# The first expert layer of a two-block model: up products of one expert between the two halves of the down products of the expert in front of it

## The chip, the cores and the metric

One core of one Trainium2 chip runs the whole program. The metric is the device time of one execution in microseconds; several executions are shown, and one more was taken with the hardware profiler.

## The reference

The program computes two transformer-like blocks on 512 tokens of width 1024, with a second stream of 256 context tokens. The change concerns one piece, the expert layer behind the first mixer of the second block (layer 0), which runs over both streams:

```python
def expert_choice_ffn(h, router, w1, w3, w2):
    B, T, D = h.shape
    cap = max(1, EC_FACTOR * T // N_EXPERTS)
    aff = jax.nn.softmax(jnp.einsum('btd,de->bte', h, router).astype(jnp.float32), -1)
    gate, idx = lax.top_k(jnp.swapaxes(aff, 1, 2), cap)
    xs = jax.vmap(lambda hb, ib: hb[ib])(h, idx)
    hid = jax.nn.silu(jnp.einsum('becd,edf->becf', xs, w1)) * jnp.einsum('becd,edf->becf', xs, w3)
    ys = jnp.einsum('becf,efd->becd', hid, w2) * gate[..., None].astype(h.dtype)
    return jax.vmap(lambda yb, ib: jnp.zeros((T, D), yb.dtype).at[ib.reshape(-1)].add(yb.reshape(-1, D)))(ys, idx)
```

There are 16 experts, each with three 1024 x 1024 fp32 matrices. With 512 tokens each expert takes cap = 64 of them, with 256 context tokens 32. The result is scaled by a modulation gate and added to the residual. All arithmetic is fp32.

## The kernel before, in words

`moe` (L1432) builds one expert layer and is called twice: for layer 0 with two token groups, group 0 with cap 64 and group 1 with cap 32 (L2601), and for layer 1 with group 0 alone (L2620). The change touches layer 0.

**Weights.** Each expert has 12 parts of 1 MB: a quarter q of w1, w3 and w2 each. `load` (L1452) issues them on SyncE's queue in the order of the list `todo` (L1441), into 14 slots that are used in turn; a load waits until both groups have used the part that was in its slot. `load(12*e + 36)` at the head of each expert names the parts that may be issued by then.

**One expert.** `up` (L1607) multiplies a quarter of w1 and w3 with the tokens xT, `act` (L1619) makes silu(h1)*h3 of the result with ScalarE and VectorE, `turned` (L1634) transposes that on TensorE and copies it to hT with ScalarE (L1640), `down` (L1643) multiplies hT with a quarter of w2 into yb, and `collect` (L1658) takes yb out: group 0 with two operations of VectorE (L1669), group 1 with four copies of ScalarE (L1672, L1673) and two additions of VectorE (L1674). Group 0's products use 64 columns of TensorE, two of them side by side; group 1's use 32, four side by side. In the trace each fp32 product is two records. h is group 0's result of the up products, hc that of group 1, and both groups' down products are yb (128\*64 for group 0, 128\*32 for group 1).

**Around the experts.** The tokens of 2 experts of group 0 (4 of group 1) are gathered together: `fetch` (L1463) finds them with a product (L1473) and an indirect DMA on POOL's queue, `turn` (L1559) transposes them into xT (L1567, evicted on L1571 and L1573), and `scatter` (L1575) brings their results back to the tokens' places: yh on ScalarE (L1588), yl and back on VectorE (L1590, L1594), products with them on TensorE (L1599), and an addition to the residual on VectorE (L1601). The scatter is a generator; `beside.step()` and `beside.drain()` run it in pieces during the up products of the next expert.

**The order.** Inside an expert the two groups are staggered: the up products run h0, h1, hc0, h2, hc1, h3, hc2 (the digit is the quarter), then act and transposes of group 0, hc3 and the act of group 1, the down products of group 0 with the transposes of group 1 in front of its third quarter, and the down products of group 1 two quarters behind. The program's order is a priority and not the order of execution: a planner goes through it once when the program is built, places on each engine the first instruction in that order whose operands are ready by its own estimate, and gives out buffers as they come free. The order that results on each engine is fixed, and is what the trace shows; this order of instructions is called the list in what follows. All products, transposes and scatters share 8 PSUM banks.

```python
            for q in range(4):
                ups(q, 0)
                if late:
                    ups(q - 1, 1)
                if q > 1:
                    beside.step()
            th = act(0, G[0])
            beside.drain()
```

Of the kernel before, what the change touches and what calls it, by code (L numbers as in the profile page):

```python
# [10 lines left out]
F32 = mybir.dt.float32  # L11
F32R = mybir.dt.float32r
BF16 = mybir.dt.bfloat16
I32 = mybir.dt.int32
# [6 lines left out]
D = 1024  # L21
# [140 lines left out]
class Feed:  # L162
# [16 lines left out]
    def load(self, upto):  # L179
        nc = self.k.nc  # L180
        while len(self.raws) < min(upto, len(self.specs)):
            src, n, w = self.specs[len(self.raws)]
            raw = self.tl("raw", F32, self.nraw, n, w)
            nc.sync.dma_start(raw, src.rearrange("(k p) c -> p k c", p=128))
            self.raws.append(raw)
# [787 lines left out]
def seg(t):  # L973

    return slice(t * 128, t * 128 + 128)
# [453 lines left out]

def moe(k, layer, groups, mods, psum, es, nslot, extra, out=None, side="right"):  # L1432

# [2 lines left out]
    bank = lambda nm="ps": psum.tile([128, 512], F32, name=nm, tag="ps")  # L1438
    dp = k.pool(f"md{layer}", 1, DRAM, es)
    parts = [("w1", 0), ("w3", 0), ("w1", 1), ("w3", 1), ("w1", 2), ("w3", 2), ("w1", 3), ("w3", 3), ("w2", 0), ("w2", 1), ("w2", 2), ("w2", 3)]  # L1440
    todo = [(e, nm, q) for e in range(16) for nm, q in parts]  # L1441
    W, pools, G, made = {}, [], [], {}

    alone = len(groups) == 1
# [18 lines left out]
    def fetch(g, gi, a):  # L1463

        n, ne, cap = g["n"], g["ne"], g["cap"]
        b = bank()
        w = 1 if alone else n
        for t in range(0, n, w):
            oh = pf.tile([128, w, ne, cap], F32, name="oh", tag=f"oh{gi}", bufs=1 + alone)
            nc.vector.tensor_tensor(oh, iota[:, :cap].unsqueeze(1).unsqueeze(1).to_broadcast([128, w, ne, cap]),  # L1470
                                    g["pos"][:, t:t + w, a * ne:a * ne + ne].unsqueeze(3).to_broadcast([128, w, ne, cap]), op=ALU.is_equal)
            for i in range(w):
                nc.tensor.matmul(b[:, :ne + 1], oh[:, i].rearrange("p e c -> p (e c)"), g["ext"][:, t + i, a], start=(t + i == 0), stop=(t + i == n - 1))  # L1473
        ii = pf.tile([128, 1], I32, name="ii", tag=f"ii{gi}", bufs=2)
        nc.vector.tensor_copy(ii, b[:, 0:1])
        xs = pf.tile([128, D], F32, name="xs", tag="xs", bufs=len(groups))
        nc.gpsimd.indirect_dma_start(out=xs, out_offset=None, in_=g["xh"][:, :],  # L1477
                                     in_offset=bass.IndirectOffsetOnAxis(ap=ii[:, 0:1], axis=0))
        sl = pf.tile([128, ne + 1], F32, name="sl", tag=f"sl{gi}", bufs=2)
        nc.vector.tensor_copy(sl, b[:, :ne + 1])  # L1480
        gate = pf.tile([128, 1], F32, name="gt", tag=f"gt{gi}", bufs=2)
        for e in range(ne):
            nc.vector.tensor_scalar(gate[e * cap:e * cap + cap], sl[e * cap:e * cap + cap, 1 + e:2 + e], 0.5, None, ALU.mult)
        return dict(xs=xs, sl=sl, gate=gate)
# [149 lines left out]
    def turned(gi, g, th):  # L1634
        m = 2 * g["cap"]
        b = bank()
        hT = p.tile([128, 4, m], F32, name="hT", tag=f"th{gi}" if alone else f"hT{gi}", bufs=1)
        for c in range(4):
            nc.tensor.transpose(b[:, c * m:c * m + m], th[:, seg(c)], k.id[:m, :m])
        nc.scalar.copy(hT.rearrange("p c m -> p (c m)"), b[:, :4 * m])  # L1640
        return hT
# [13 lines left out]
                    o, first, last = 64 * dh + 32 * (i % 2), i < 2, i > 5  # L1655
                nc.tensor.matmul(yb[o:o + cap], lhs, w[:, j, dh * 512:dh * 512 + 512], start=first, stop=last, tile_position=(0, o))  # L1656

    def collect(e, gi, g, yb):  # L1658

        cap = g["cap"]  # L1660
        ei = e % g["ne"]
        if ei == 0:
            cur[gi]["ys"] = p.tile([128, D], F32, name="ys", tag=f"ys{gi}", bufs=1)
        ys = cur[gi]["ys"]
        so = slice(ei * cap, ei * cap + cap)
        for dh in range(2):
            ds_ = slice(dh * 512, dh * 512 + 512)
            if cap == 64:
                nc.vector.tensor_tensor(ys[so, ds_], yb[64 * dh:64 * dh + 64], g["gate"][so, ds_], op=ALU.mult)  # L1669
            else:  # L1670
                t = p.tile([128, 512], F32, name="yt", tag="yt", bufs=1)
                nc.scalar.copy(ys[so, ds_], yb[64 * dh:64 * dh + 32])  # L1672
                nc.scalar.copy(t[so], yb[64 * dh + 32:64 * dh + 64])  # L1673
                nc.vector.tensor_tensor(ys[so, ds_], ys[so, ds_], t[so], op=ALU.add)  # L1674

    def run():
        nonlocal rp, pf, pq, p, iota, tid, one, hb
        slots()
        rp = k.pool(f"mr{layer}", 1, None, es)
        iota = rp.tile([128, 128], F32, name="iota")  # L1680
        nc.gpsimd.iota(iota, pattern=[[1, 128]], base=0, channel_multiplier=0, allow_small_or_imprecise_dtypes=True)
        tid = rp.tile([128, 6], F32, name="tid")
        nc.gpsimd.iota(tid, pattern=[[128, 6]], base=0, channel_multiplier=1, allow_small_or_imprecise_dtypes=True)
        for gi, g in enumerate(G):
            g["gate"] = mods.gate(g["r"], 1, rp, f"g2{layer}{gi}")
        if extra:
            pools.append(k.pool(f"mv{layer}", 1, None, es))
        load(nslot + extra - (2 if extra else 6))
        pf = k.pool(f"mf{layer}", 1, None, es)
        with ExitStack() as e2:  # L1690
            pq = k.pool(f"mq{layer}", 1, None, e2, "left")
            one = pq.tile([16, 512], F32, name="one")
            nc.gpsimd.memset(one, 1.0)
            chosen = [choose(gi, g) for gi, g in enumerate(G)]
            while any(g is None for g in nxt):
                for c in chosen:
                    next(c, 0)
        load(nslot + extra, nc.gpsimd)
        load(24)
        p = k.pool(f"mx{layer}", 1, None, es)  # L1700
        for gi, g in enumerate(G):
            turn(g, gi, nxt[gi])
        for e in range(16):
            load(12 * e + 36)
            for gi, g in enumerate(G):
                if e % g["ne"] == 0:
                    cur[gi] = nxt[gi]
            hb = [[bank("h1"), bank("h3")] if g["cap"] == 64 else [bank("hc")] for g in G]
            ybs, hTs, late = [bank("yb") for _ in G], [None] * len(G), len(G) - 1

            def ups(q, gi):
                if 0 <= q < 4:
                    up(e, q, gi, G[gi])

            def downs(q, gi):
                if 0 <= q < 4:
                    down(e, q, gi, G[gi], hTs[gi], ybs[gi])
# [10 lines that stand above are left out]
            for gi, g in enumerate(G):  # L1728
                if e % g["ne"] == g["ne"] - 2 and e < 16 - 2:
                    nxt[gi] = fetch(g, gi, e // g["ne"] + 1)  # L1730
            hTs[0] = turned(0, G[0], th)
            if late:
                ups(3, 1)
                th = act(1, G[1])
            for q in range(4 + 2 * late):
                downs(q, 0)
                if late and q == 1:
                    hTs[1] = turned(1, G[1], th)
                if late:
                    downs(q - 2, 1)  # L1740
                if q == 1:
                    for gi, g in enumerate(G):
                        if e % g["ne"] == g["ne"] - 1 and e < 15:
                            turn(g, gi, nxt[gi])
            for gi, g in enumerate(G):
                collect(e, gi, g, ybs[gi])
                if e % g["ne"] == g["ne"] - 1:
                    beside.add(scatter(g, cur[gi], e == 15))
        beside.drain()
        es.close()  # L1750

    rp = pf = pq = p = iota = tid = one = hb = None
    cur, nxt = [None] * len(groups), [None] * len(groups)
    beside = Side()
# [825 lines left out]
def whole(tc, I, out):  # L2580
    nc = tc.nc
    with ExitStack() as es:
        k = K(tc, I, es)
        setup(k)
        psum = k.pool("ps", 8, PSUM)
# [3 lines left out]
        mods = [Mods(k, i, mp, dr) for i in range(2)]  # L2589
# [8 lines left out]
        c = k.pool("xc", 1, None, ex, "left").tile([128, 2, D], F32, name="cres")  # L2598
        nc.sync.dma_start(c, I["ctx_2"][0].rearrange("(t p) d -> p t d", p=128))
        xt, ct = [x[:, t] for t in range(4)], [c[:, t] for t in range(2)]  # L2600
        first = moe(k, 0, [(0, xt, 64), (1, ct, 32)], mods[0], psum, ExitStack(), 14, 0, side="left")  # L2601
        def both(p):
            for a in range(2):
                yield from mods[1].make(psum, p, 128, 6, a)
# [44 lines left out]
```

## Time and profile before

| | us |
|---|---|
| Runs shown | 3454.38, 3463.92, 3468.79 (median 3463.92) |
| Profiled execution, its own time | 3452.15 |
| Span of the profiled execution | 3450.3 |
| First expert layer, first up product to last down product | 1523.2 to 2135.5 |

The span runs from the first to the last instruction of the profiled execution; its own time is 1.85 us longer. Times in the rows are us from the start of the span unless they say ns. In a row of the timeline the columns are start, duration from the first start to the last end, engine, line and operation, the tile written and those read, shape, and the number of records that follow one another without another group between; a bracket gives the idle time of the engine before it and what ended it. PE is TensorE, DVE VectorE, ACT ScalarE, POOL GpSimd, SPq the queue of SyncE. A later block's start less an earlier one's is the time that the earlier one took, since ends of products are modelled.

### The profile page before, as it was taken

How to read it: one execution, taken by the hardware profiler on the slowest of the kernel's cores; microseconds unless marked ns; L12 is line 12 of the kernel's file. 1: busy time of each engine (PE TensorE's matmuls, PEld its weight loads, DVE VectorE, ACT ScalarE, POOL GpSimd, SP SyncE). 2: the span in 40 equal slices, each digit the busy share in tenths (PEclk: the TensorE clock that was granted, in tenths of full speed). 3: DMA queues.
4: the chain of work that ended last, by engine and by line, in shares of the span. 5: the costliest groups of instructions: out<-in, count | busy, mean ns of one | idle time of the engine just before them, and what ended most of it. 6: DMA issues, size and time to landing. Idle time of an engine off the chain costs nothing.

```text
span 3450.3 us, 52389 instructions
## 1 busy us (share of the span) xinstructions
PE 3103.6 (90%) x21072; PEld 2032.6 (59%) x21072; DVE 1538.3 (45%) x3435; ACT 1013.0 (29%) x2175; POOL 975.3 (28%) x859
## 2 busy tenths in 40 slices
PE   8999999998989899979999999899768579699888
PEld 6898778886768666743333333687647467333322
DVE  3233544414378687342323334331577776332212
ACT  4333333322212454211111212222557443011000
POOL 5342434332323552410000000424646344000000
PEclk9999999999989999979999999899879779899999
DMA  4121122225257232178888884343222234799998
GB/s 145 61 74 49 62 74 70 66 68 166 93 158 203 81 101 65 49 304 339 333 341 334 333 339 166 105 140 117 80 59 71 66 96 154 311 409 409 409 409 349
DMA packets 372552, 625.94 MB, mean 181 GB/s; under 512 B 43998, under 2 KB 240525, under 8 KB 372310
## 3 DMA queue, kind: packets, MB, share of 16 engines
q1 hardware_dynamic: 367190, 603.58, 49.2%
q0 software_dynamic: 5120, 19.01, 1.5%
q8 instruction: 167, 2.74, 0.3%
q14 instruction: 75, 0.61, 0.1%
HBM read 596.61 MB, written 25.91 MB: 180 GB/s over the span
## 4 chain that ended last, share of the span: by engine, by line
PE 73%; DVE 11%; DMA 8%; ACT 4%; issue 2%; POOL 2%; SPq 1%; POOLq 0%; DVEq 0%; ACTq 0%
PE ps L102 11%; PE h L1617 10%; PE ps L103 10%; PE ps L104 10%; PE yb L1656 7%; DMA w<-in_moe_w_dram 6%; PE hc L1617 4%; PE ps L1599 2%; PE ps L926 1%; PE ob L762 1%; PE ps L2253 1%; DVE acc L1100 1%; DVE pr L2308 1%; DVE N L2309 1%; PE ob L1303 1%
## 5 line engine op out<-in xcount | busy, mean ns | idle before, releaser
L201 POOL TENSOR_TENSOR wlo<-wraw,whi 128x1024 fp32r<-128x1024 f32 (+5 forms) x219 | 426.8, 1970 | 755.2 <-ACT whi L197 736.5
L1617 PE MATMUL h<-w,xT 128*64 128x512 f32 x2048 | 462.6, 597 | 23.7 <-DMA w<-in_moe_w_dram 18.1
L1617 PEld LDWEIGHTS h<-w,xT 128*64 128x64 f32 x2048 | 141.1, 137 | 335.0 <-issue 253.9
L1656 PE MATMUL yb<-w,hT 128*64 128x512 f32 (+1 forms) x1536 | 301.0, 599 | 17.8 <-ACT hT L1640 15.4
L197 ACT CAST whi<-wraw 128x2048 fp32r<-128x2048 f32 (+4 forms) x108 | 161.5, 1495 | 235.7 <-PE ps L103 111.8
L1477 POOL DMA_INDIRECT xs<-xh,ii x20 | 21.3, 1067 | 728.9 <-DVE sl L1480 708.6
L1625 DVE SCALAR_TENSOR_TENSOR th<-th,h 128x512 f32<-128x512 f32 x32 | 22.0, 688 | 413.3 <-ACT th L1624 413.3
L1656 PEld LDWEIGHTS yb<-w,hT 128*64 128x64 f32 (+1 forms) x1536 | 87.2, 128 | 197.3 <-issue 153.6
L102 PE MATMUL ps<-hT,whi 128*128 128x512 f32 x416 | 171.2, 412 | 0.0
L102 PE MATMUL ps<-whi,hT 128*128 128x512 f32 (+1 forms) x424 | 164.3, 388 | 4.9 <-DVE hT L316 2.7
L103 PE MATMUL ps<-hT,wlo 128*128 128x512 f32 x416 | 166.3, 400 | 0.0
L1624 ACT ACTIVATE th<-h 128x512 f32<-128x512 f32 x32 | 19.1, 597 | 499.7 <-PE h L1617 499.7
L104 PE MATMUL ps<-hT,whi 128*128 128x512 f32 x416 | 165.7, 398 | 0.0
L103 PE MATMUL ps<-whi,hT 128*128 128x512 f32 (+1 forms) x424 | 156.4, 369 | 0.0
L104 PE MATMUL ps<-wlo,hT 128*128 128x512 f32 (+1 forms) x424 | 154.5, 367 | 0.0
L115 POOL TENSOR_TENSOR rs<-rs_t,mhalf 128x8 f32<-128x8 f32 (+3 forms) x78 | 94.7, 1218 | 113.5 <-DVE rs_t L110 93.7
L1617 PE MATMUL hc<-w,xT 128*32 128x512 f32 x1024 | 124.2, 598 | 0.0
L1669 DVE TENSOR_TENSOR ys<-yb,g 64x512 f32<-64x512 f32 x64 | 44.1, 688 | 177.5 <-PE yb L1656 177.0
L102 PEld LDWEIGHTS ps<-whi,hT 128*128 128x128 f32 x424 | 104.3, 246 | 14.5 <-DVE hT L316 3.2
L103 PEld LDWEIGHTS ps<-whi,hT 128*128 128x128 f32 x424 | 104.6, 247 | 6.4 <-issue 1.9
L1100 DVE SCALAR_TENSOR_TENSOR acc<-glu,w,acc 128x798 f32<-128x798 f32 x90 | 106.6, 1221 | 1.0
L104 PEld LDWEIGHTS ps<-wlo,hT 128*128 128x128 f32 x424 | 103.9, 246 | 5.2 <-issue 0.2
(810 smaller groups left out, 6831.4 us busy)
## 6 DMA issues: line engine op xcount, KB each, us to landing
w<-in_moe_w_dram SPq DMA_DIRECT2D x376, 1024.0 KB
wraw<-in_w_in_dram SPq DMA_DIRECT2D x48, 1024.0 KB
aw<-in_ada_w_dram SPq DMA_DIRECT2D x192, 256.0 KB
wraw<-in_od_w_in_dram SPq DMA_DIRECT2D x27, 512.0 KB
rows<-rw_rows SPq DMA_DIRECT2D x48, 192.0 KB
w<-in_moe_w_dram POOLq DMA_DIRECT2D x8, 1024.0 KB, 10.0
xh<-xn SPq DMA_DIRECT2D x10, 512.0 KB
wraw<-in_w_proj_b_dram SPq DMA_DIRECT2D x4, 1024.0 KB
```

The source lines that it names most:

```text
L102: nc.tensor.matmul(out, L[0], R[0], start=start, stop=False)
L103: nc.tensor.matmul(out, L[1], R[0], start=False, stop=False)
L104: nc.tensor.matmul(out, L[0], R[1], start=False, stop=stop)
L115: nc.gpsimd.tensor_tensor(out, t, mh.to_broadcast(list(ss.shape)), op=ALU.pow)
L197: nc.scalar.copy(hi, raw)
L201: eng.tensor_tensor(lo[:, a:b], raw[:, a:b], hi[:, a:b].bitcast(F32), op=ALU.subtract)
L762: nc.tensor.matmul(ob[pp, m * 128:m * 128 + 128], vs[a], pT[:, 2 * j + a], start=(a == 0), stop=(a == 1))
L1100: v.scalar_tensor_tensor(acc[:, c], glu[:, c, j:j + W], w2[:, j, c:c + 1], acc[:, c], ALU.mult, ALU.add)
L1599: nc.tensor.matmul(b, back, y[:, hs], start=(i == 0), stop=(i == len(terms) - 1))
L1617: nc.tensor.matmul(bb[o:o + cap], lhs, w[:, kk % 2, fh * 512:fh * 512 + 512], start=(kk == 0), stop=(kk == 7), tile_position=(0, o))
L1656: nc.tensor.matmul(yb[o:o + cap], lhs, w[:, j, dh * 512:dh * 512 + 512], start=first, stop=last, tile_position=(0, o))
L1669: nc.vector.tensor_tensor(ys[so, ds_], yb[64 * dh:64 * dh + 64], g["gate"][so, ds_], op=ALU.mult)
```

## The change

For layer 0 `moe` is called with `apart=True`. Then the expert loop is replaced by `staggered`, which runs 17 rounds. Round e has, in this order: the up products of expert e, quarter by quarter, both groups in step; the activations of both; the fetch for the next tokens and the rest of a scatter; quarters 2 and 3 of the down products of expert e-1 in step, and its collect; the transposes of both groups of expert e; quarters 0 and 1 of its down products; and the transposes of the next tokens where they are due. The weights' list follows that order of use: w1 and w3 of e, quarters 2 and 3 of w2 of e-1, quarters 0 and 1 of w2 of e. hT has two buffers, and ii, sl and the gate of the gathered tokens three. `collect` is given the gathered tokens it belongs to.

```diff
-def moe(k, layer, groups, mods, psum, es, nslot, extra, out=None, side="right"):
+def moe(k, layer, groups, mods, psum, es, nslot, extra, out=None, side="right", apart=False):
...
+    if apart:
+        todo = []
+        for e in range(17):
+            todo += [(e, nm, q) for nm, q in parts[:8] if e < 16] + [(e - 1, "w2", q) for q in (2, 3) if e] + [(e, "w2", q) for q in (0, 1) if e < 16]
...
-        ii = pf.tile([128, 1], I32, name="ii", tag=f"ii{gi}", bufs=2)
+        ii = pf.tile([128, 1], I32, name="ii", tag=f"ii{gi}", bufs=2 + apart)
...
-        hT = p.tile([128, 4, m], F32, name="hT", tag=f"th{gi}" if alone else f"hT{gi}", bufs=1)
+        hT = p.tile([128, 4, m], F32, name="hT", tag=f"th{gi}" if alone else f"hT{gi}", bufs=2 if apart else 1)
...
-        for e in range(16):
+        if apart:
+            staggered()
+        for e in range(0 if apart else 16):
...
+    def staggered():
+
+        nonlocal hb
+        before = None
+        for e in range(17):
+            load(12 * e + 36)
+            if e < 16:
+                for gi, g in enumerate(G):
+                    if e % g["ne"] == 0:
+                        cur[gi] = nxt[gi]
+                hb = [[bank("h1"), bank("h3")] if g["cap"] == 64 else [bank("hc")] for g in G]
+                for q in range(4):
+                    for gi, g in enumerate(G):
+                        up(e, q, gi, g)
+                    if q > 1:
+                        beside.step()
+                th = [act(gi, g) for gi, g in enumerate(G)]
+                for gi, g in enumerate(G):
+                    if e % g["ne"] == g["ne"] - 2 and e < 16 - 2:
+                        nxt[gi] = fetch(g, gi, e // g["ne"] + 1)
+            beside.drain()
+            if before:
+                hTs, ybs, cs = before
+                for q in (2, 3):
+                    for gi, g in enumerate(G):
+                        down(e - 1, q, gi, g, hTs[gi], ybs[gi])
+                for gi, g in enumerate(G):
+                    collect(e - 1, gi, g, cs[gi], ybs[gi])
+                    if (e - 1) % g["ne"] == g["ne"] - 1:
+                        beside.add(scatter(g, cs[gi], e == 16))
+            if e < 16:
+                hTs = [turned(gi, g, th[gi]) for gi, g in enumerate(G)]
+                ybs = [bank("yb") for _ in G]
+                before = hTs, ybs, list(cur)
+                for q in (0, 1):
+                    for gi, g in enumerate(G):
+                        down(e, q, gi, g, hTs[gi], ybs[gi])
+                for gi, g in enumerate(G):
+                    if e % g["ne"] == g["ne"] - 1 and e < 15:
+                        turn(g, gi, nxt[gi])
...
-        first = moe(k, 0, [(0, xt, 64), (1, ct, 32)], mods[0], psum, ExitStack(), 14, 0, side="left")
+        first = moe(k, 0, [(0, xt, 64), (1, ct, 32)], mods[0], psum, ExitStack(), 14, 0, side="left", apart=True)
```

## Rows read from the trace of the kernel before

**Rows 1.** The page: length of the profiled span.
```profile
span 3450.3 us, 52389 instructions
```
**Rows 2.** Windows: busy time of each engine from first up to last down product.
```profile
core 0: us, PE busy (x) PEld busy (x) DVE busy (x) ACT busy (x) POOL busy (x), PEclk, DMA share, GB/s
1523.20:2135.50 612.30, 599.43 (x3486) 204.77 (x3485) 172.93 (x337) 108.07 (x196) 18.30 (x13) 1.00 0.84 322
```
**Rows 3.** Timeline of TensorE: expert 1, and the first block of expert 2.
```profile
1559.79 7.09 PE L1617 MATMUL h<-w,xT 128*64 128x512 f32 x32
1566.81 1.94 PE L1617 MATMUL hc<-w,xT 128*32 128x512 f32 x16
1568.68 3.65 PE L1617 MATMUL h<-w,xT 128*64 128x512 f32 x16
...
1577.71 3.66 PE L1617 MATMUL hc<-w,xT 128*32 128x512 f32 x32
1581.31 0.66 PE L1639 MATMUL ps<-cc,th 128*128 128x128 f32 x4
1582.64 7.08 PE L1656 MATMUL yb<-w,hT 128*64 128x512 f32 x30 [0.67 <-ACT hT L1640]
1589.65 0.46 PE L1639 MATMUL ps<-cc,th 64*128 64x64 f32 x4
1590.04 1.09 PE L1567 MATMUL ps<-cc,xs 128*128 128x128 f32 x8
1591.06 4.64 PE L1656 MATMUL yb<-w,hT 128*64 128x512 f32 x34
1595.63 0.65 PE L1617 MATMUL h<-w,xT 128*64 128x512 f32 x2
```
**Rows 4.** Waits in 1523 to 2150: us in total, times, longest us.
```profile
PE yb L1656 <- ACT hT L1640: 8.6, 13, 0.8
```
**Rows 5.** Timeline of TensorE: end of expert 0's up products; last torn block.
```profile
1544.01 1.90 PE L1617 MATMUL hc<-w,xT 128*32 128x512 f32 x6
1545.85 0.65 PE L1639 MATMUL ps<-cc,th 128*128 128x128 f32 x4
1546.43 1.92 PE L1617 MATMUL hc<-w,xT 128*32 128x512 f32 x10
...
2130.89 4.64 PE L1656 MATMUL yb<-w,hT 128*64 128x512 f32 x34
```
**Rows 6.** Timeline of TensorE: scatter waits of expert 12, hT wait of expert 14.
```profile
2010.70 0.74 PE L1599 MATMUL ps<-yh,back 128*128 128x512 f32 x2 [1.06 <-ACT yh L1588]
2011.80 0.73 PE L1599 MATMUL ps<-yh,back 128*128 128x512 f32 x2 [0.35 <-DVE back L1594]
...
2088.67 7.08 PE L1656 MATMUL yb<-w,hT 128*64 128x512 f32 x30 [0.75 <-ACT hT L1640]
```
**Rows 7.** Timeline of all engines: ScalarE's collect copies, then transposes and hT, expert 5.
```profile
1714.56 7.09 PE L1617 MATMUL h<-w,xT 128*64 128x512 f32 x32
1714.69 0.57 ACT L1672 COPY ys<-yb 32x512 f32<-32x512 f32 x1 [6.81 <-PE yb L1656]
...
1715.88 0.58 ACT L1672 COPY ys<-yb 32x512 f32<-32x512 f32 x1
...
1736.07 0.66 PE L1639 MATMUL ps<-cc,th 128*128 128x128 f32 x4
...
1736.77 0.58 ACT L1640 COPY hT<-ps 128x512 f32<-128x512 f32 x1
```
**Rows 8.** Timeline of all engines: the end of the layer, first scatter operand and product.
```profile
2133.43 1.15 ACT L1588 ACTIVATE yh<-ys,gt 128x1024 fp32r<-128x1024 f32 x1 [2.06 <-DVE ys L1669]
...
2135.47 1.21 PE L1599 MATMUL ps<-yh,back 128*128 128x512 f32 x4
```
**Rows 9.** Waits of SyncE's queue in 1470 to 2150: us in total, times, longest us.
```profile
SPq L1458 <- PE hc L1617: 333.6, 61, 49.6
```
**Rows 10.** The instructions of the tile w, its last line: time of one load.
```profile
DMA to landing us min/median/max: 6.0/10.0/16.6
```

More of the change, by code (lines that the diff above doesn't have):

```diff
@@ L1478, in fetch @@
                                      in_offset=bass.IndirectOffsetOnAxis(ap=ii[:, 0:1], axis=0))
-        sl = pf.tile([128, ne + 1], F32, name="sl", tag=f"sl{gi}", bufs=2)
+        sl = pf.tile([128, ne + 1], F32, name="sl", tag=f"sl{gi}", bufs=2 + apart)
         nc.vector.tensor_copy(sl, b[:, :ne + 1])
-        gate = pf.tile([128, 1], F32, name="gt", tag=f"gt{gi}", bufs=2)
+        gate = pf.tile([128, 1], F32, name="gt", tag=f"gt{gi}", bufs=2 + apart)
         for e in range(ne):
@@ L1656, in down, with collect @@
                 nc.tensor.matmul(yb[o:o + cap], lhs, w[:, j, dh * 512:dh * 512 + 512], start=first, stop=last, tile_position=(0, o))
-    def collect(e, gi, g, yb):
+    def collect(e, gi, g, c, yb):
         cap = g["cap"]
@@ L1662, in collect @@
         if ei == 0:
-            cur[gi]["ys"] = p.tile([128, D], F32, name="ys", tag=f"ys{gi}", bufs=1)
-        ys = cur[gi]["ys"]
+            c["ys"] = p.tile([128, D], F32, name="ys", tag=f"ys{gi}", bufs=1)
+        ys = c["ys"]
         so = slice(ei * cap, ei * cap + cap)
@@ L1745, in run @@
             for gi, g in enumerate(G):
-                collect(e, gi, g, ybs[gi])
+                collect(e, gi, g, cur[gi], ybs[gi])
                 if e % g["ne"] == g["ne"] - 1:
```

## Prediction

> **What bounds the kernel now.** I read the page first, for the span [rows 1], then the windows for the stretch of the first expert layer [rows 2], then TensorE's instructions in order of time within it. [...] So TensorE bounds the layer, and what counts is how its 38.3 us per expert (612.3/16) are made up.
>
> One expert without a scatter shows it [rows 3]: from 1559.79 to 1595.63, 35.84 us. Two blocks of the same shape differ by 16 records and 3.44 us (7.09 - 3.65); two products of group 0 (64 columns each) run side by side, so that is 8 slots of 0.43 us. A slot of group 1 holds four records. A block of 32 takes 7.02 us to the next block's start, that is 16 x 0.43 + 0.14; a block of 16 of group 1 takes 1.87, 4 x 0.43 + 0.15. So each change of shape costs some 0.14 us beside the slots, and the order of the groups is not free. This expert has six such blocks in its up products and three in its down products.
>
> Three things in it are waste. After the transposes of group 0 (line 1639) TensorE waits 0.67 us for ScalarE's copy hT; in the whole layer that is 8.6 us in 13 waits [rows 4]. The down products of group 0 come as x30 and, behind the transposes of group 1, x34: a pair was torn, and two products run alone. x30 takes 7.02 us to the next start, as a full x32 does, and x34 takes 4.57 where 1 + 8 slots and two changes would be 4.15; on both sides together 18 slots of group 0 were used for 16, 0.86 us. Twelve experts are torn like that, the last at 2130.89, and the first expert's up products of group 1 once: 6 records take 1.84 us, four slots, and the other 10 four more, where 16 need four: 1.7 us [rows 5]. And in three experts (4, 8, 12) TensorE waits 1.06 + 0.35 us for the scatter's operands [rows 6].
>
> **What the change removes.** With the down products of the expert in front (its second half) standing behind the up products, the activations of both groups have some 5.7 us of cover (4 blocks: 12 slots x 0.43 + 4 x 0.14), the two transposes can stand together, and the scatter's waits have other work. If all three wastes go: 8.6 + 12 x 0.86 + 1.7 + 3 x 1.41 = 24.8 us. This is the most that can come off, because the products, transposes, scatters and fetches are all still there.
>
> **What it adds in changes of shape.** Group 0 and group 1 now alternate at each quarter: 8 blocks in the up products, 4 + 4 in the down products, 16 instead of 9. 7 x 16 experts x 0.14 = 15.7 us. Between 0 (the list merges blocks again, a rival) and 17.9 (at 0.16, if the small blocks pay more) I take 15.7, from [rows 3]. [...]
>
> **The wait that takes the place of the old one.** hT of group 0 is now made right after the collect of the expert in front. In the profile, ScalarE's copies of group 1's yb begin 0.13 us after the last down product and follow at 0.60 us each (1714.69 to 1715.88 for two), four to an expert; the transposes' result reaches ScalarE 0.70 us after their start [rows 7]. So at the time the copy hT could begin, ScalarE has collect copies, which stand ahead in the program. With TensorE's own 0.97 us for both transposes (0.58 [rows 5] + 0.39 [rows 3]): with ScalarE free the wait left over is 1.33 - 0.97 = 0.36 us. With two copies ahead hT begins at 1.32, ends at 1.90, and the wait is 1.0 us; with three it is 1.6. The trace of before has no such meeting; I take the middle, 1.0. In seven odd experts the next tokens' transposes (line 1567, 1.02 us for one group [rows 3]) can stand in it, so it counts in nine: 9.0 us; ends 3.2 (0.36 x 9) and 25 (1.6, nearly everywhere). Behind the waiting product stands everything else on TensorE, and with it the release of weight slots. That TensorE fills the wait with the next expert's up products is not what I expect: it did not in the 0.75 us at 2088.67 [rows 6], though that expert's tokens need no new transposes.
>
> **The scatter and the banks.** yb of both groups now lives through the next up products: 2 + 3 of the 8 banks, so that 3 are free for the scatter, where before yb was first written after it and 5 were free. The scatter's later products also become ready in the middle of the down products, and whoever is interrupted pays two changes and a torn pair, 2 x 0.14 + 0.86 = 1.1 us. Once in each of the seven scatters inside the layer: 8.0 us; bounds 0 (no interruption) and 16 (two in each).
>
> **The ends.** In the last expert group 0's down products now end only 1.0 us ahead of the last ones, where before its yh started 2.04 us ahead of the scatter's first product and was ready for it [rows 8]; I charge 2 us, bounds 0 and 3. In the first expert nothing covers the activations: group 0's chain ends inside group 1's last block, and group 1's inside group 0's down products; 0, at most 1.
>
> **What costs nothing.** SyncE's order of loads follows the new order of use. Its queue waits 333.6 us for group 1's up products to give slots back [rows 9], so the weights wait for slots and not TensorE for weights. A slot is used again 14 parts later, 14 x 612.3/192 = 45 us, and a part lands in 10.0 us [rows 10]. If that cover went, the price would be the bandwidth: at 0.84 busy, DMA would allow 612.3 x 0.84 = 514 us. Indirect loads on POOL are moved behind the activations by a few us and are needed an expert later. The third buffers of ii, sl and the gate, and the second hT, copy nothing.
>
> **The sum.** -24.8 + 15.7 + 9.0 + 8.0 + 2.0 = +9.9 us. The profiled execution took 3452.15 us, with 1.85 around its span; by the sum it would take 3462. It lies 11.8 below the median of the three runs, 3463.92; on that median the forecast is 3474, 0.3% more. A measurement of this kernel can tell about 0.5% (17 us) from no change, so I call it no change, leaning to slower. The forecast's own range, with the low ends of the wait and the scatter (-24.8 + 15.7 + 3.2 = -5.9), is 3458 to 3481.
>
> **The rivals.** *ScalarE's copies become the bound* (slower). Place: between the transposes and the first down product of each expert. Three copies ahead of hT, and no cover: 15 x 1.6 = 24, and the rest of the sum is +0.9, so +25, 3489 us. It decides from a wait of about 1.0 us in all sixteen experts ((17.3 - 0.9)/16). For it: the program's order, and that ready work of other experts was not pulled forward before. Against it: the list can put hT into the gap in which the fourth copy waits for VectorE. [...] 35%.
>
> *The order gives merged blocks* (faster). As x32 of group 1 shows [rows 3], the list puts neighbours of one shape together when something between them is not ready. With two extra changes instead of seven (4.5 us), hT waiting 0.36 and whole scatters: -24.8 + 4.5 + 3.2 = -17; with none, -22: about 3444. Against it: in the up products every operand is there, and the list followed the program's order there in all sixteen experts. 17%.
>
> *The change does not do what it says.* The list is free to move group 1's products back behind group 0's, and the order of before comes out nearly whole; then the time is within 5 us of before, 3464. The trace shows moves of a few us, not of a whole half. 8%.
>
> **How the numbers follow.** My forecast has the remaining 40%, and the third rival lies in the same band: no change 48%, slower 35%, faster 17%. The range reaches from 3448, near the faster rival, to 3499, which takes in the slower rival and 10 us of its scatters' upper bound; about one in ten is left out on either side.
>
> **What would show it.** Right: in TensorE's timeline blocks of x16 and x16 in turn in the up products and of x8 in the down products, some 16 to an expert; an idle time ahead of yb put down to ScalarE's hT of about 1 us, with collect copies just before that copy; no x30 and x34. A layer of 608 to 630 us. Wrong: blocks of x32 still there; hT waits under 0.4 us; a layer under 595 us; or TensorE waiting for weights, which nothing above prices.

## The result: 1.1% slower, and the profile after

| | before | after |
|---|---|---|
| median | 3461.51 us (3454.38 to 3468.79, 4 runs) | 3501.48 us (3489.07 to 3504.14, 4 runs) |
| ratio after to before | | 1.0108, 95% interval [1.0076, 1.0141] |
| profiled execution: span | 3450.3 us | 3498.9 us |
| layer, first up product to the start of the last down product | 611.7 us | 645.0 us |
| blocks of one line and shape on TensorE in it | 215 | 301 |
| of these, blocks of up and down products | 152 | 227 |
| slots that the up and down products take (1152 if every pair and every four is whole) | 1180 | 1198 |

Blocks and slots are counted from the starts of the records in the trace. A slot here is a set of products of one shape that start within 0.12 us of each other. A row of the timeline can hold blocks of both groups, because both write yb.

The forecast was 3474 us with a range up to 3499; the change came out 2 us above that range, on the side that had 35%. Of the 48.6 us between the two spans, 33.3 lie inside the layer and 3 right behind it. 8.7 lie in front of it, where TensorE, VectorE, ScalarE and GpSimd have the same instructions in the same order in both kernels: the layer starts at 1523.2 us in the one profile and at 1531.9 in the other, and in the profiles of the kernels below anywhere from 1522.2 to 1536.5. They are no part of the change; some 3.5 more lie further behind the layer. The medians, 40 us apart, agree with the 36 in the layer and right behind it.

The windows of the changed kernel over its layer, with the columns of [rows 2]:

```profile
1531.90:2177.00 645.10, 622.52 (x3485) 200.44 (x3484) 170.72 (x335) 106.32 (x195) 18.57 (x13) 0.99 0.81 305
```

TensorE is busy 23 us longer than in [rows 2] with the same products, and waits 10 us more. The starts of the records divide the layer's 33.3 us up, to 0.2 us:

- Waits: 9.7 us more.
- Torn pairs and fours: 18 slots more at 0.43 us, 7.7 us.
- Changes of shape: the first and last slots of the product blocks take 22.5 us beyond 0.43 each before and 32.4 after. That is 0.148 and 0.143 us a block, and 9.9 us more.
- Slots inside a block that ran long: 1.6 us before and 5.1 after, 3.4 more. Most of the 5.1 lies behind waits of more than 1 us, in slots of 0.85 us at a granted clock of 0.50; the 1.6 of before stands at 1779, behind a wait of 0.67 us, at 0.50 as well.
- Transposes, fetches and scatters: 2.4 us more.

The waits of TensorE in the same stretch (us in total, times, longest us), where [rows 4] had 8.6 us for hT alone:

```profile
PE ps L1644 <- DVE th L1636: 14.3, 7, 3.2
PE yb L1661 <- ACT hT L1645: 5.1, 7, 1.6
PE ps L1604 <- ACT yh L1593: 3.2, 3, 1.1
```

The largest of them is new and stood at nothing in the forecast: the transposes of group 1's th wait for VectorE. TensorE's timeline around one of the longest, at 1879.31, from an odd expert's end into the next round:

```profile
1837.07 8.08 PE L1661 MATMUL yb<-w,hT 128*64 128x512 f32 x42 [0.28 <-ACT hT L1645]
1845.08 1.96 PE L1572 MATMUL ps<-cc,xs 128*128 128x128 f32 x16
1846.97 3.91 PE L1661 MATMUL yb<-w,hT 128*32 128x512 f32 x18
1850.81 4.50 PE L1622 MATMUL h<-w,xT 128*64 128x512 f32 x18
1855.25 1.94 PE L1622 MATMUL hc<-w,xT 128*32 128x512 f32 x16
1857.12 3.65 PE L1622 MATMUL h<-w,xT 128*64 128x512 f32 x14
...
1874.45 1.05 PE L1661 MATMUL yb<-w,hT 128*32 128x512 f32 x4
1875.43 0.66 PE L1644 MATMUL ps<-cc,th 128*128 128x128 f32 x4
1879.31 0.69 PE L1644 MATMUL ps<-cc,th 64*128 64x64 f32 x4 [3.22 <-DVE th L1636]
1879.92 8.48 PE L1661 MATMUL yb<-w,hT 128*64 128x512 f32 x40
```

Three things are to be seen. The up products alternate in x16 and x16, as forecast. The second half of the down products, which should stand behind the next expert's ups, has been pulled ahead of them: 60 of this expert's 64 records of down products run before the ups (the x42 at 1837.07, and the x18 at 1846.97 behind the turn of new tokens), and just four are left at 1874.45 as cover. And an up block is torn: two blocks of 16 records became x18 and x14, and the x14 takes 3.65 us, as a whole x16 does in [rows 3]. What the transposes really wait for shows on ScalarE and VectorE in the same stretch:

```profile
1875.55 0.57 ACT L1677 COPY ys<-yb 32x512 f32<-32x512 f32 x1 [1.31 <-PE yb L1661]
1876.14 0.57 ACT L1678 COPY yt<-yb 32x512 f32<-32x512 f32 x1
1876.74 0.58 ACT L1677 COPY ys<-yb 32x512 f32<-32x512 f32 x1
1877.34 0.58 ACT L1645 COPY hT<-ps 128x512 f32<-128x512 f32 x1
1877.95 0.58 ACT L1635 COPY h3s<-hc 64x512 f32<-64x512 f32 x1
...
1878.57 0.68 DVE L1636 TENSOR_TENSOR th<-th,h3s 64x512 f32<-64x512 f32 x1 [1.13 <-ACT h3s L1635]
```

VectorE itself waits for ScalarE's h3s, and h3s stands behind three collect copies and a copy hT. Where the cover is there, the same three copies stand ahead of hT instead, as here at the start of expert 1's down products:

```profile
1593.49 0.57 ACT L1677 COPY ys<-yb 32x512 f32<-32x512 f32 x1 [3.82 <-PE yb L1661]
1594.08 0.58 ACT L1678 COPY yt<-yb 32x512 f32<-32x512 f32 x1
1594.68 0.58 ACT L1677 COPY ys<-yb 32x512 f32<-32x512 f32 x1
1595.28 0.86 ACT L1645 COPY hT<-ps 128x512 f32<-128x512 f32 x2
1595.92 2.37 PE L1661 MATMUL yb<-w,hT 128*64 128x512 f32 x10 [1.57 <-ACT hT L1645]
```

Behind the layer, the scatter's first product waits where it did not in [rows 8]:

```profile
2179.39 1.15 ACT L1593 ACTIVATE yh<-ys,gt 128x1024 fp32r<-128x1024 f32 x1
...
2180.59 2.08 PE L1604 MATMUL ps<-yh,back 128*128 128x512 f32 x4 [3.06 <-ACT yh L1593]
```

### The profile page after: what moved, and what is told of

It reads as the page before. It is cut to its first block, busy times and chain, and to the rows that moved or that the text cites. A ratio compares the mean times of both kernels' runs of the same rounds, so it can differ in the third digit from the quotient of the medians.

```text
span 3498.9 us, 52378 instructions
## 1 busy us (share of the span) xinstructions
PE 3145.2 (90%) x21072; PEld 2041.0 (58%) x21072; DVE 1537.7 (44%) x3435; ACT 1012.5 (29%) x2175; POOL 977.1 (28%) x859
## 4 chain that ended last, share of the span: by engine, by line
PE 74%; DVE 10%; DMA 8%; ACT 4%; issue 2%; POOL 2%; SPq 1%; ACTq 0%; DVEq 0%; POOLq 0%
PE ps L102 11%; PE h L1622 10%; PE ps L103 10%; PE ps L104 10%; PE yb L1661 8%; DMA w<-in_moe_w_dram 5%; PE hc L1622 4%; PE ps L1604 2%; PE ps L926 1%; PE ob L762 1%; DVE pr L2356 1%; PE ps L2301 1%; DVE acc L1100 1%; PE ob L1303 1%; DVE N L2357 1%
## 5 line engine op out<-in xcount | busy, mean ns | idle before, releaser
L1622 PE MATMUL h<-w,xT 128*64 128x512 f32 x2048 | 472.3, 602 | 22.5 <-DMA w<-in_moe_w_dram 17.0
L1661 PE MATMUL yb<-w,hT 128*64 128x512 f32 (+1 forms) x1536 | 313.7, 605 | 14.2 <-ACT hT L1645 11.8
L1482 POOL DMA_INDIRECT xs<-xh,ii x20 | 21.6, 1081 | 888.6 <-DVE sl L1485 791.6
```

Source lines behind the costliest of these rows:

```text
L1622: nc.tensor.matmul(bb[o:o + cap], lhs, w[:, kk % 2, fh * 512:fh * 512 + 512], start=(kk == 0), stop=(kk == 7), tile_position=(0, o))
```

## Experiments

The planner that lists each engine's instructions moves them as it finds them ready, so most edits hold something back: `issue_after(i)` puts what its block traces on the engine of i behind i (in all_hold yh, at 1781.59, stands behind the hT copies of 1780.85). All results, against runs of the kernel before; layer, blocks, slots and waits are counted as above, each from one profile ("th" and "hT": TensorE's waits for each; in the expectations T0 and T1 are the transposes of group 0 and of group 1):

| kernel | layer us | blocks | slots | th / hT us | ratio to before, interval |
|---|---|---|---|---|---|
| before | 611.7 | 215 | 1180 | 0 / 8.6 | 1 |
| after | 645.0 | 301 | 1198 | 14.3 / 5.1 | 1.0108 [1.0076, 1.0141] |
| merge | 629.8 | 209 | 1176 | 13.7 / 5.7 | 1.0062 [1.0042, 1.0083] |
| pin | 651.1 | 299 | 1184 | 2.0 / 21.6 | 1.0125 [1.0101, 1.0150] |
| tfirst | 644.7 | 301 | 1198 | 14.3 / 5.1 | 1.0109 [1.0078, 1.0139] |
| split | 769.4 | 428 | 1446 | 13.1 / 4.9 | 1.0470 [1.0447, 1.0493] |
| pin_hold | 632.4 | 316 | 1212 | 2.0 / 3.4 | 1.0078 [1.0058, 1.0098] |
| merge_pin | 624.8 | 199 | 1170 | 2.0 / 18.5 | 1.0026 [1.0011, 1.0042] |
| merge_hold | 614.4 | 201 | 1164 | 10.2 / 1.9 | 0.9996 [0.9979, 1.0013] |
| all_hold | 602.5 | 199 | 1170 | 2.0 / 3.4 | 0.9989 [0.9979, 0.9998] |
| whole_hold | 597.1 | 167 | 1170 | 2.0 / 3.4 | 0.9968 [0.9954, 0.9982] |
| untorn | 603.3 | 216 | 1156 | 0 / 8.2 | 0.9988 [0.9974, 1.0001] |
| untorn_whole | 594.4 | 157 | 1164 | 0 / 0 | 0.9940 [0.9922, 0.9957] |

**merge: two quarters of a group together.** This undoes most of the alternation. The scatter's steps, which stood behind the third and the fourth quarter, move behind the ups.

```diff
-                for q in range(4):
+                for q in (0, 2):
                     for gi, g in enumerate(G):
-                        up(e, q, gi, g)
-                    if q > 1:
-                        beside.step()
+                        for i in range(2):
+                            up(e, q + i, gi, g)
+                beside.step(2)
...
-                for q in (2, 3):
-                    for gi, g in enumerate(G):
+                for gi, g in enumerate(G):
+                    for q in (2, 3):
```

(the last edit also for the quarters 0 and 1)

> Two quarters of a group stand together, in the up products and in each half of the down products: 8 blocks to an expert instead of 16, nothing else. Theory B (0.14 us for each change of shape): 128 changes less, 18 us, layer 645.0 to 625-630. Theory A (the cover): the number of blocks is not what counts, waits stay, layer 640-645.

3482.20 us; the layer loses 15.2 us with 92 blocks fewer, while the waits stay (13.7 and 5.7). The quotient, 0.165 us a block, is not the price of a change of shape, because the edit did more: fewer pairs and fours are torn, 22 slots or 9.4 us; the ends of 83 product blocks fewer give 11.2; scatters, fetches and transposes give 1.0; and slots inside the blocks, behind the waits, run 6.5 us longer. The number of blocks counts, as theory B says, but it was not alone in this run.

**pin: the second half of the down products held behind the ups.**

```diff
-                        up(e, q, gi, g)
+                        last = up(e, q, gi, g)
...
-                for q in (2, 3):
-                    for gi, g in enumerate(G):
-                        down(e - 1, q, gi, g, hTs[gi], ybs[gi])
+                with k.tc.issue_after(last):
+                    for q in (2, 3):
+                        for gi, g in enumerate(G):
+                            down(e - 1, q, gi, g, hTs[gi], ybs[gi])
```

> The order of issue on TensorE is held: the second half of an expert's down products stands behind the next expert's last up product. If the pulled-forward half is what cost the cover (theory A): the waits of group 1's transposes for VectorE, 14.3 us in 7 rounds, fall below 2; the torn groups of group 1's down products go, some 6 us; in their place the waits for hT come back in the even rounds, 5.1 to 12-15 us, and the next tokens stand uncovered, up to 1 us in 7 rounds. Layer of 645.0 us to 630-640. If the changes of shape are the loss (theory B): waits may move, but the layer stays within 4 us of 645.

3506.99 us. The waits for th fell to 2.0 us, as expected, and 21.6 us of waits for hT took their place. The loss had only moved: 14 slots fewer, the 6 us expected for torn groups, did come off, but the waits together grew by 4.3 us and slots inside the blocks ran 6.5 us longer. The layer of 651.1 us is what neither theory had expected. ScalarE and TensorE in one round of it:

```profile
1883.90 0.57 ACT L1678 COPY ys<-yb 32x512 f32<-32x512 f32 x1 [4.75 <-PE yb L1662]
1884.49 0.57 ACT L1679 COPY yt<-yb 32x512 f32<-32x512 f32 x1
1885.09 0.58 ACT L1678 COPY ys<-yb 32x512 f32<-32x512 f32 x1
...
1885.69 1.15 ACT L1593 ACTIVATE yh<-ys,gt 128x1024 fp32r<-128x1024 f32 x1
1886.87 0.86 ACT L1646 COPY hT<-ps 128x512 f32<-128x512 f32 x2
...
1887.51 2.02 PE L1662 MATMUL yb<-w,hT 128*64 128x512 f32 x6 [2.70 <-ACT hT L1646]
```

**tfirst: `turned` traced ahead of `collect`.**

```diff
+                if e < 16:
+                    hTs = [turned(gi, g, th[gi]) for gi, g in enumerate(G)]
                 for gi, g in enumerate(G):
                     collect(e - 1, gi, g, cs[gi], ybs[gi])
...
```

> The transposes of an expert stand ahead of the collect of the expert in front in the program, so that ScalarE's copy hT comes ahead of the collect's four copies. If ScalarE's copies are what hT waits for (theory C): waits for hT, 5.1 us in 7 rounds, fall below 2.5 and no wait of 1.5 us is left; layer 641-642. By A and B alone: no change, 645 within 2.

3503.85 us, with the same order of instructions on TensorE, ScalarE and VectorE in the layer as in the changed kernel. The program's order of these two steps did not reach ScalarE's queue, so this did not test the theory; pin_hold does. It shows how well a layer repeats: 644.7 us for 645.0, with the same waits.

**split: the groups alternate after each of w1 and w3.** Meant to double the changes of shape in the up products.

```diff
-                        up(e, q, gi, g)
+                        up(e, q, gi, g, (wi,))
```

(under a loop over wi, and `up` skips the other matrix)

> The suspected cost doubled: in the up products the groups alternate after each matrix (w1, w3) of a quarter instead of after each quarter, 8 more changes of shape to an expert, 128 in the layer, the same products. Theory B: +18 us at 0.14 us each, layer 663. Theory A: only small, 645-650.

3621.64 us, far above every expectation, and the edit was not clean: four products of group 1 run side by side, two of w1 and two of w3. With the matrices apart only two do, and group 1's up products take 510 slots for 264 and 234.8 us for 123.4. Group 0's up products, whose pairs stay whole, come nearer to the price that was asked for: 64 more blocks, 6.5 us, 0.10 each.

**pin_hold: pin, and ScalarE's collect copies and yh behind the hT copies.**

```diff
+        made["hT"] = nc.scalar.copy(hT.rearrange("p c m -> p (c m)"), b[:, :4 * m]).ins
...
+                if e < 16:
+                    hTs = [turned(gi, g, th[gi]) for gi, g in enumerate(G)]
+                with k.tc.issue_after(made["hT"]):
+                    for gi, g in enumerate(G):
+                        collect(e - 1, gi, g, cs[gi], ybs[gi])
+                        if (e - 1) % g["ne"] == g["ne"] - 1:
+                            beside.add(scatter(g, cs[gi], e == 16))
+                            if gi == 0:
+                                beside.step()
```

> The kernel 'pin' (second half of the down products held behind the last up product of the next expert) plus an order for ScalarE: group 1's collect copies, and the first step of group 0's scatter with its copy yh, are queued behind the two hT copies of the round. Theory E (ScalarE's own order makes the hT waits: what stands ahead of the hT copies there is collect and yh): the hT waits of 'pin', 21.6 us, fall to about 6 us, the slow product blocks behind the waits of 2.7 us disappear with them, and the layer's 651 us become about 630, the time about 3487 us, ratio 1.005 to before. Rival F (a wait between the turn of th and the next down product is there whatever ScalarE does, a good 1 us for transposes, copy and signals): the waits stay above 14 us, the layer above 641, the time above 3497.

3484.98 us. The hT waits fell from 21.6 to 3.4 us and the layer from 651.1 to 632.4. ScalarE's order is what made them; the rival needed a layer above 641. The 18.7 us are a net figure: the waits lose 21.4 us and the slots inside the blocks 11.2, while group 1's up products, torn more often, take 28 slots more, 12.0 us. The scatters stand in 34 pieces there for 24.

**merge_pin, merge_hold, all_hold: the two edits on top of merge, each alone and together.** merge_pin has the hold of the down products, merge_hold the hold on ScalarE, all_hold both.

> 'merge' (layer 629.8 us) plus the hold of the second half of the down products alone, without the order for ScalarE. If the cover and ScalarE's order are two halves of one wait (T1's wait for VectorE before, the hT wait behind the scatter's yh after), the hold alone only moves the loss, as in 'pin' against the change (645.0 to 651.1): T1 waits fall from 13.7 to about 2 us, hT waits rise from 5.7 to about 21, layer 628 to 636, ratio 1.005 to 1.008. Rival: the waits came of the many pieces, and with the blocks merged the hold alone gives back the 11 us of T1 waits: layer 619 or less, ratio 1.003 or less.

> 'merge' (layer 629.8 us) plus the order for ScalarE alone, without the hold of the down products. If the two belong together, this alone takes only the hT waits of 5.7 us down to 2 or 3, and the T1 waits of 13.7 us stay, since the products that covered them are still pulled ahead: layer 624 to 629, ratio 1.004 to 1.006. Rival: ScalarE's copies are behind all of it (th, h3s and the copies go through the same queue): the T1 waits go too and the layer falls under 612, ratio 1.000.

> The two quarters of a group stand together (as in 'merge'), the second half of the down products is held behind the next ups (as in 'pin'), and ScalarE's collect copies and yh stand behind the hT copies. If the loss of the change is the sum of its changes of shape (15 us by 'merge'), of the covers eaten and of ScalarE's order (together 19 us of waits, of which some 6 stay, and the pairs torn by pulled products), the three together give the loss of the layer back: about 614 us against 612 before, ratio 0.999 (0.995 to 1.003). If one of them had only moved elsewhere (the clock, or weights that come late), the layer stays above 622 and the ratio above 1.004.

merge_pin: 3473.12 us; again nearly all of the wait moved (13.7 + 5.7 became 2.0 + 18.5), and 5.0 us came off, a little more than expected. merge_hold: 3465.88 us, 15.4 us off the layer, more than expected and less than its rival asked: the hT waits fall to 1.9 and the th waits to 10.2, 7.4 together, and group 1's up products also take 5.8 us less, 12 slots. all_hold: 3456.00 us, 602.5 us, 12 us below what was expected. Merged blocks, the cover and ScalarE's order together give back 42.5 us, and the changed loop is then shorter than before by 9.2.

merge_pin and all_hold have the same instructions in the same order on TensorE, and the edit between them is ScalarE's order, so the cost of a wait can be read beside its absence. The same round of merge_pin (timeline, then windows of 2 us from the wait's end on, columns as in [rows 2]):

```profile
1789.84 1.15 ACT L1593 ACTIVATE yh<-ys,gt 128x1024 fp32r<-128x1024 f32 x1 [4.47 <-DVE ys L1675]
...
1792.82 0.86 ACT L1646 COPY hT<-ps 128x512 f32<-128x512 f32 x2
1793.46 7.21 PE L1662 MATMUL yb<-w,hT 128*64 128x512 f32 x32 [2.27 <-ACT hT L1646]
```
```profile
1793.40:1795.40 2.00, 1.94 (x8) 0.72 (x10) 0.68 (x1) 0.86 (x3) 0.00 (x0) 0.80 1.02 414
1795.40:1797.40 2.00, 2.00 (x6) 0.48 (x4) 0.00 (x0) 0.00 (x0) 0.00 (x0) 0.50 1.03 416
1797.40:1799.40 2.00, 2.00 (x14) 0.53 (x14) 0.00 (x0) 0.00 (x0) 0.00 (x0) 0.84 1.01 406
```

and of all_hold:

```profile
1780.85 0.86 ACT L1646 COPY hT<-ps 128x512 f32<-128x512 f32 x2 [5.47 <-PE ps L1645]
1781.49 5.51 PE L1662 MATMUL yb<-w,hT 128*64 128x512 f32 x32 [0.29 <-ACT hT L1646]
1781.59 1.16 ACT L1593 ACTIVATE yh<-ys,gt 128x1024 fp32r<-128x1024 f32 x1
```
```profile
1783.40:1785.40 2.00, 2.00 (x14) 0.44 (x12) 1.35 (x2) 1.72 (x3) 0.00 (x0) 1.00 1.01 403
```

With yh and the copies behind hT the wait is 0.29 us for 2.27, and the 32 records behind it take 5.51 for 7.21: after the long wait the granted clock falls to 0.50 and stands at 0.84 two us later. Over the layer the 15.1 us more of hT wait in merge_pin come with 7.0 us more in group 0's down products (123.7 us against 116.7), which accounts for 22.1 of the 22.3 us between the two layers.

**whole_hold: as all_hold, all four quarters of a group's ups together.**

```diff
-                for q in (0, 2):
-                    for gi, g in enumerate(G):
-                        for i in range(2):
-                            last = up(e, q + i, gi, g)
+                for gi, g in enumerate(G):
+                    for q in range(4):
+                        last = up(e, q, gi, g)
```

> As 'all_hold', but all four quarters of a group's up products stand together: 32 changes of shape fewer than there, at 0.15 us each 5 us, so a layer of about 608 us and a ratio of 0.997, if nothing else binds. Rival: the eight weight tiles of an expert's ups come free only when group 1 has used them, half an expert later, with 14 tiles in all; then TensorE waits for weights (up products waiting for DMA, which no kernel so far shows), and the layer is longer than that of 'all_hold', 625 us or more.

3450.28 us; 5.4 us for 32 blocks, 0.168 each, with the same slots and waits: this is the cleanest pair of runs for the price of a change. TensorE waits for no weights in the layer, although their buffers are held longer; that rival is out.

**untorn: the kernel before, with the torn pair mended.** In its loop over the experts:

```diff
-            for q in range(4 + 2 * late):
-                downs(q, 0)
...
+            for q in range(3):
+                last = down(e, q, 0, G[0], hTs[0], ybs[0])
+            with k.tc.issue_after(last):
                 if late:
+                    hTs[1] = turned(1, G[1], th)
...
+            with k.tc.issue_after(made["T"]):
+                down(e, 3, 0, G[0], hTs[0], ybs[0])
+            if late:
+                for q in range(4):
+                    down(e, q, 1, G[1], hTs[1], ybs[1])
```

(`made["T"]` is the last transpose of `turned`; the turn of the next tokens stands with it)

> The kernel before, changed in one place: group 1's th is turned behind the third quarter of group 0's down products and their last quarter is held behind that turn, so that no side-by-side pair of products is torn by it. The pairs torn in before were read as 12 x 0.86 us; the last quarter (8 products, 1.7 us) covers group 1's hT copy. By the price of a slot, 0.43 us, and of a change of shape, 0.14 us, the layer's 612 us become about 603, ratio 0.997 (0.995 to 0.999). Rival: the torn products were the cover of the hT wait and their time returns as wait: layer 610 to 613, ratio 1.000.

3457.90 us; the layer loses 8.4 us, close to what was read from [rows 3] (12 x 0.86 = 10.3): exactly 24 slots are gone, 10.3 us, and the scatters, fetches and transposes take 1.4 more. The time moves by less than can be told apart from nothing.

**untorn_whole: untorn, with a group's ups together.** Group 1's ups stand behind group 0's, with group 0's transposes in their middle; no product crosses to another expert.

```diff
             for q in range(4):
                 ups(q, 0)
-                if late:
-                    ups(q - 1, 1)
...
+                up(e, 0, 1, G[1])
+                last = up(e, 1, 1, G[1])
+                with k.tc.issue_after(last):
+                    hTs[0] = turned(0, G[0], th)
+                with k.tc.issue_after(made["T"]):
+                    for q in (2, 3):
+                        ups(q, 1)
```

> The kernel before with 'untorn' and with all four quarters of a group's up products together, group 1's turn of th for group 0 in the middle of group 1's ups; no down product crosses to another expert. It asks whether having the next expert's ups between the halves of the downs is worth anything by itself. 'untorn' has 603.3 us for the layer and 216 blocks, this has about 64 blocks fewer, at 0.165 us each 10.6 us: layer 593 us, ratio 0.996, that is as good as 'whole_hold' (597.1 us, 0.9968): the interleaving itself is worth no more than the hT wait of about 0.7 us per expert. Rival: without products of another expert the turn of th waits again (T0 behind VectorE's th, hT behind its copy): layer 600 or more, worse than 'whole_hold'.

3441.52 us, the fastest kernel here, 0.6% below before. Its expert 1 on TensorE, beside [rows 3]:

```profile
1557.02 13.95 PE L1617 MATMUL h<-w,xT 128*64 128x512 f32 x64
1570.91 3.66 PE L1617 MATMUL hc<-w,xT 128*32 128x512 f32 x32
1574.50 0.66 PE L1640 MATMUL ps<-cc,th 128*128 128x128 f32 x4
1575.09 3.66 PE L1617 MATMUL hc<-w,xT 128*32 128x512 f32 x32
1578.68 5.37 PE L1657 MATMUL yb<-w,hT 128*64 128x512 f32 x24
1583.98 0.46 PE L1640 MATMUL ps<-cc,th 64*128 64x64 f32 x4
1584.38 1.09 PE L1567 MATMUL ps<-cc,xs 128*128 128x128 f32 x8
1585.40 5.51 PE L1657 MATMUL yb<-w,hT 128*64 128x512 f32 x40
1590.84 13.95 PE L1617 MATMUL h<-w,xT 128*64 128x512 f32 x64
```

33.82 us for 35.84, with no wait in it: each hT copy is covered by products of the same expert. The rival, that products of another expert are needed for that, is out: the layer's only waits are the scatters', 6.4 us. The interleaving, even in the best order tried (whole_hold, 597.1 us), was not worth more than this.

## Why the prediction leaned the right way and came out too low

The lean to slower was right, and so were two of the signs that were named for it: the alternating blocks of x16, and hT behind collect copies. The sum was too small: +9.9 us, where layer and tail grew by 36, and the layer of 645 us lies above the 608 to 630 that were named. "No change" was called at a mark of 0.5%; the measured 1.1% is beyond it. Step by step, against the layer's +33.3:

- **The step that failed first: "the activations of both groups have some 5.7 us of cover".** Waits for th had no price, and they cost 14.3 us. Two parts of the step were wrong. The list pulled the covering products ahead of the ups after odd experts, a move of a whole half, which the third rival had been held unlikely for; pin puts them back, and the wait goes. And the collect copies were charged only where they stand ahead of hT; they stand ahead of h3s as well, and with the cover back (pin) yh stands behind them, ahead of hT. Cover and queue are one wait with two places, as merge_pin shows; only the two holds together bring it down (all_hold, 2.0 and 3.4 us).
- **The second step that failed: torn pairs, -12.0, with scatter interruptions, +8.0.** Together -4.0, and 18 torn slots more made it +7.7. The 28 slots too many of before did not go; they became 46. x30 and x34 are gone, but other blocks are torn (x18 and x14 above), and the scatters stand in 24 pieces for 17. The pulled half accounts for a part: pin has 14 slots fewer, 6.0 us. What tears the rest was not followed. That the pairs of before cost what was read is shown by untorn.
- **Changes of shape, +15.7: the price right, the number too high.** There are 75 more blocks of products (86 of all kinds) instead of 112, and they cost 9.9 us, 12.3 with the 2.4 us of transposes, fetches and scatters. [Rows 3] gave 0.14; the block ends of the two traces give 0.148 and 0.143. whole_hold, with 32 blocks fewer than all_hold, gives 0.168.
- **The hT waits, -8.6 and +9.0: the right place, too narrow.** They went from 8.6 to 5.1, 3.5 better than before, where the sum had +0.4; hT did meet three collect copies (1.57 us against the 1.6 reckoned).
- **The scatter's waits, -4.2: mostly not removed.** The waits for yh are 3.2 us in three, before and after alike; those for `back`, 1.1, are gone.
- **The clock, in no term: 3.4 us** of slots that ran long, most of them behind the new waits: those of 2.00, 1.71 and 3.22 us at 1558, 1795 and 1879 are followed by 3.2 us at a granted clock of 0.50, another of 3.22 us at 2044 by 1.00.
- **The tail, +2.0:** the wait is 3.06 us, the upper bound; the scatter's last product comes 2.5 us later than before. Weights, DMA and buffers at nothing: right, TensorE waits for none of them in the layer.

That the time ended only 2 us above the range is in part luck: fewer changes of shape and shorter hT waits took 7 us off errors of 32.

The slower rival named ScalarE's copies as the bound, and the holds show that they are one of two causes of the new waits, beside the lost cover. Its 3489 fell short by the th waits, the torn products and the clock. It had its price for one place in ScalarE's queue, and the range was built on that.

## What to carry to other kernels

Before products are moved as cover, follow every instruction on the way from the covered result to its consumer through its engine's queue, and count what the move puts ahead of each: here a small copy (h3s) two steps up decided, not the copy that feeds TensorE. Where a planner orders ready work, a cover is there only if it is held there (the waits for th are 13.7 us in merge, 2.0 in merge_pin), and holding one half of a chain moved the wait to the other half (hT, 5.7 to 18.5). Count the slots too: a pair that something else interrupts cost 0.86 us in the kernel before, a wait for hT 0.67. And try first whether the old order, with its blocks merged and its pairs whole, gives the gain without the move: it did here.

## What was not expected of the hardware

A wait of 2.3 us cost TensorE more than its length here: the clock granted after it was 0.80, 0.50 and 0.84 in three windows of 2 us, and 32 records took 7.21 us for 5.51. A wait of 0.29 us in the same place left it at 1.00. And products of 32 columns side by side took almost twice the slots where only two of the four came together: 510 for 264, and 234.8 us for 123.4.
